# Splits read from PSUM, a negation from raw weights, and one scaling per conv block in a one-core decoder trunk

## The chip, the cores and the metric

The kernel runs on one core of one Trainium2 chip. The metric is device time in microseconds for one launch; the kernel before takes 1084.95 us (median of three runs, 1084.92 to 1085.11).

The core has five engines that run their own instruction queues in order: TensorE (matmuls; PE in the profile, PEld its weight loads), VectorE (DVE), ScalarE (ACT), GpSimd (POOL) and SyncE (SP, which here only issues transfers). SBUF is the on-chip memory, PSUM the accumulators that matmuls write.

## The reference

One layer of a decoder trunk on 288 token columns: 256 positions of a new sequence and 8 x 4 new tokens of running sequences.

```python
h = rmsnorm(x, norm1_g)
proj = einsum("btd,de->bte", h, w_in) + b_in          # 2048 -> 3072
a, gate, z = proj[..., :1024], proj[..., 1024:2048], proj[..., 2048:]
u = a * sigmoid(gate)
c = silu(layernorm(depthwise_causal_conv([hist_conv, u], conv_w, conv_b)))   # 31 taps
# pooling: 4 groups of 256 channels with windows 2, 4, 8, 16
d = window_sum([hist_pool, z]) / count - z
p = einsum("btgc,gce->btge", d, pool_w) * pool_scale                         # 256x256 a group
x = x + einsum("btm,md->btd", concat([c, p]), w_out)                         # 2048 -> 2048
f = square(relu(einsum("btd,df->btf", rmsnorm(x, norm2_g), w_ff1)))          # 2048 -> 8192
x = x + einsum("btf,fd->btd", f, w_ff2)                                      # 8192 -> 2048
y = rmsnorm(x, norm_f)
```

The last 30 conv inputs and 15 pooling inputs of each sequence are outputs too.

## The kernel before, in words

Channels lie on the 128 partitions, the 288 tokens along the free dimension (`T`). Every matmul is 128x128 weights by 128x288 activations in fp32r, a shortened fp32. To keep the precision, each operand is held as two parts, `hi` (the value rounded to fp32r) and `lo` (value minus `hi`), and each product is made of three matmuls: hi by hi, lo by hi, hi by lo. TensorE does 8176 matmuls, and everything else has to make operands in time.

**Weights.** `load` brings a block of 1024 rows by 256 columns as two raw tiles of 4 k blocks each (here called quarters, since two blocks, so four such tiles, make one column pair of 2048 rows). A quarter serves 24 matmuls. `split_part` (L254) makes `hi` and `lo`. `hi` is a copy on ScalarE (L260). `lo` is made in one of three ways, by the letters in `WAYS` (L73), one letter per quarter:

- "V": VectorE subtracts `hi` from raw (L265).
- "G": GpSimd does, in two halves of 128x512 (L269).
- "D": ScalarE writes the negated `hi` into `lo` (L262), and then a transfer from DRAM that adds to its destination brings raw once more (L263). GpSimd issues these transfers.

There are 6 raw tiles and 5 pairs of `hi` and `lo` tiles, used in turn: a quarter is split when the quarter five earlier has been used up by TensorE.

**Order.** `SEQUENCE` (L38) sets the order of the first stage: c0 to c7 are the eight conv column pairs, p3 to p0 the projections of the four pooling groups, P3 to P0 the pooling products of 12 matmuls each. TensorE runs them in the order written: c0 to c4, p3, c5, p2, P3, c6, p1, P2, p0, c7 with P1 inside, then the first columns of w_out with P0 inside, and so on to the feed-forward matrices. A c or p block is 96 matmuls. The order on the other engines is laid out by a planner that simulates durations when the kernel is built and lets ready work of higher rank go first; the conv taps (L459, 31 multiply-adds per block on VectorE, with products for the new tokens on GpSimd, L463) have the lowest rank. Each queue then runs in that fixed order.

**A conv block** (`conv_pair`, L429): both PSUM halves are scaled by the norm's factor `rb` (L434), the gate half goes through the sigmoid (L436), and u is formed (L438). **A pooling group** (`pool_group`, L476): the projection is scaled (L482) and biased on ScalarE (L485, L486), GpSimd adds shifted copies to get window sums `s` (L491) and forms the difference for the new tokens (L497, L498), VectorE the one for the sequence (L500); then `d` is split into `dh` (ScalarE, L502) and `dl` (VectorE, L503). `pool_products` (L509) multiplies them by the pool weights and splits the result again (L514, L515).

**The `ms` tile.** `ms()` hands out one PSUM tile of two banks with a single buffer: each user waits until the one before has been read. Before the change its users around the pooling are only the four pooling products, and the sums of the norms.

`pool_weights` (L375) loads and splits the 256x256 weights of one group; it is called one group ahead of its use, at the end of the block before on TensorE.

Of the kernel before, what the change touches and what calls it, by code (L numbers as in the profile page):

```python
# [9 lines left out]
F32 = mybir.dt.float32  # L10
# [6 lines left out]
P = 128  # L17
# [9 lines left out]
PH = 15  # L27
# [42 lines left out]
TURN = "110100" * 4 + "01" * 6 + "1100" * 3  # L70


WAYS = {"c2": "GVGV", "c3": "GDGG", "c4": "GGGD", "c5": "GDGD", "c6": "GDGV", "c": "GGGV", "p0": "GDVG", "p": "GDDG", "w0": "GV", "w": "GG", "ff": "VV"}  # L73


VEC = (("norm1_g", 16), ("b_in", 24), ("conv_b", 8), ("ln_g", 8), ("ln_b", 8), ("pool_scale", 8), ("norm2_g", 16), ("norm_f", 16))
# [10 lines left out]
def trunk_kernel(ctx: ExitStack, tc: tile.TileContext, io):  # L87
# [18 lines left out]
    def nm(s):  # L106
        seen[s] = seen.get(s, 0) + 1
        return f"{s}{seen[s]}"
# [25 lines left out]
    def f32(t):  # L134
        return t.bitcast(F32)
# [118 lines left out]
    def split_part(raw, src, hi, lo, way):  # L254

        nc.scalar.copy(hi, raw)  # L260
        if way == "D":
            nc.scalar.activation(lo, f32(hi), AF.Copy, scale=-1.0)  # L262
            added.append(nc.gpsimd.dma_start(lo, src, accum_op=ALU.add))  # L263
        elif way == "V":
            nc.vector.tensor_tensor(lo, raw, f32(hi), op=ALU.subtract)  # L265
        else:
            for j in range(0, raw.shape[1], 2):
                with tc.issue_after(pooled[-1].ins) if pooled else nullcontext():
                    nc.gpsimd.tensor_tensor(lo[:, j : j + 2, :], raw[:, j : j + 2, :], f32(hi[:, j : j + 2, :]), op=ALU.subtract)  # L269
# [27 lines left out]
    def gemm(banks, rhs, m_outer=False, between={}, classes="", by_part=False, gets=None, pairs=None, late=0):  # L297


        n = len(rhs)  # L300
        gets = gets or ready.pop(0)
        todo, begins = [], {}
        if by_part:
            for k in range(0, n, 2):
                sets = [range(len(banks))] if k else [range(2), range(2, len(banks))]
                for last, ms_ in enumerate(sets, 1 - len(sets)):
                    for part, (w, x) in enumerate(((0, 0), (1, 0), (0, 1))):
                        if last == 0:
                            begins[len(todo)] = (k, None, k + 1)[part]
                        todo += [(k + (1 - d if x else d), m, w, x) for m in ms_ for d in range(2)]  # L310
        else:
            pairs = pairs or [(k, m) for k in range(0, n, 2) for m in range(len(banks))]
            if m_outer:
                pairs.sort(key=lambda km: km[1])
            for k, m in pairs:
                begins[len(todo)] = (k, m) if m else k
                todo += [(k + d, m, w, x) for d, w, x in ((0, 0, 0), (1, 0, 0), (0, 1, 0), (1, 1, 0), (1, 0, 1), (0, 0, 1))]
        todo[:late] = sorted(todo[:late], key=lambda p: p[2])
        head = todo[: len(classes)]
        for j, c in enumerate(classes):  # L320
            todo[j] = next(p for p in head if c == "." or (p[0] + p[3]) % 2 == int(c))
            head.remove(todo[j])
        ends = {m: [f(j for j, p in enumerate(todo) if p[1] == m) for f in (min, max)] for m in range(len(banks))}
        ahead = None
        for j, (k, m, w, x) in enumerate(todo):
            if begins.get(j) in between:
                ahead = between[begins[j]]()
            with tc.issue_after(ahead.ins) if ahead is not None and not chain else nullcontext():
                last = mm(banks[m][:, :T], gets[k // 8](k % 8, m)[w], rhs[k][x], start=j == ends[m][0], stop=j == ends[m][1])
        ready.extend(itertools.islice(weights, 1))  # L330
        return last.ins

    def bank2():
        return acc.tile([P, 2, 512], F32, name=nm("ac"), tag="ac")

    def each(bk):
        return [bk[:, m, :] for m in range(2)]
# [36 lines left out]

    def pool_weights(g):  # L375
        raw, (hi, lo) = load_pool(g), spl()
        split_part(raw[:, 0:2, :], None, hi[:, 0:2, :], lo[:, 0:2, :], "V")
        return lambda k, m: columns(hi, lo, k, m)

    def weight_groups():  # L380
# [41 lines left out]

    def conv_products(i, **kw):
        history(i)
        banks = each(bank2())
        gemm(banks, hx, **kw)
        return banks

    def conv_pair(i, banks):  # L429
        up = u_all[:, i, 0:UO]  # L430
        us = samples(u_all[:, i, UO:UL], US)
        ta, gate = [b[:, :T] for b in banks]
        for b in (gate, ta):
            nc.vector.tensor_tensor(b, b, rb, op=ALU.mult)  # L434
        tg = tmpp.tile([P, 2, T], F32, name=nm("tg"), tag="ag", bufs=2)[:, 0, :]
        nc.scalar.activation(tg, gate, AF.Sigmoid, bias=v("b_in", 8 + i))  # L436
        for out, a, b in ((up[:, CH:UO], ta[:, :SEQ], tg[:, :SEQ]), (us[:, :, CH:US], samples(ta[:, SEQ:T], NS), samples(tg[:, SEQ:T], NS))):
            nc.vector.scalar_tensor_tensor(out=out, in0=a, scalar=v("b_in", i), in1=b, op0=ALU.add, op1=ALU.mult)  # L438
        if i % 2 == 0:
            cs.append(actp.tile([P, 2, T], F32, name=nm("c"), tag="c", bufs=4))  # L440
        while waiting:
            taps(*waiting.pop())
        if i in (2, 3):
            waiting.append((i, up, us))
        else:
            taps(i, up, us)
# [24 lines left out]
                    nc.gpsimd.tensor_tensor(sum_c[:, 0, :], sum_c[:, 0, :], part, op=ALU.add)  # L471


    dd = {}

    def pool_group(g):  # L476
        nc.sync.dma_start(z_all[:, 2 * g : 2 * g + 2, ZO:ZL], io["hist_p"][:, 2 * g : 2 * g + 2, :])
        bk = bank2()
        gemm(each(bk), hx)
        z = z_all[:, 2 * g : 2 * g + 2, :]  # L480
        tz = tmpp.tile([P, 2, T], F32, name=nm("tz"), tag="ag", bufs=2)
        nc.vector.tensor_tensor(tz, bk[:, :, :T], both(rb), op=ALU.mult)  # L482
        for m in range(2):
            b_in = v("b_in", 16 + 2 * g + m)
            nc.scalar.activation(z[:, m, PH:ZO], tz[:, m, 0:SEQ], AF.Identity, bias=b_in)  # L485
            nc.scalar.activation(samples(z[:, m, ZO:ZL], ZS)[:, :, PH:ZS], samples(tz[:, m, SEQ:T], NS), AF.Identity, bias=b_in)  # L486
        s, w = z, 1
        while w < WINDOWS[g]:
            s2 = tmpp.tile([P, 2, ZL], F32, name=nm("s"), tag="s", bufs=2)
            for m in range(2):  # L490
                nc.gpsimd.tensor_tensor(s2[:, m, 2 * w - 1 :], s[:, m, 2 * w - 1 :], s[:, m, w - 1 : ZL - w], op=ALU.add)  # L491
            s, w = s2, 2 * w
        d = tmpp.tile([P, 2, T], F32, name=nm("d"), tag="ag2", bufs=2)
        first_sums = s[:, :, PH : PH + w - 1]
        nc.gpsimd.tensor_tensor(first_sums, first_sums, rcnt[:, None, w - 2 : 2 * w - 3].to_broadcast([P, 2, w - 1]), op=ALU.mult)
        news = [x[:, :, ZO:ZL].rearrange("p m (b t) -> p m b t", t=ZS)[:, :, :, PH:] for x in (s, z)]
        nc.gpsimd.tensor_scalar(news[0], news[0], 1.0 / w, None, op0=ALU.mult)  # L497
        last = nc.gpsimd.tensor_tensor(d[:, :, SEQ:T].rearrange("p m (b t) -> p m b t", t=NS), news[0], news[1], op=ALU.subtract)  # L498
        newest[g] = last
        nc.vector.scalar_tensor_tensor(out=d[:, :, 0:SEQ], in0=s[:, :, PH:ZO], scalar=1.0 / w, in1=z[:, :, PH:ZO], op0=ALU.mult, op1=ALU.subtract)  # L500
        dh, dl = act2("dx", tag="p", bufs=4)
        nc.scalar.copy(dh, d)  # L502
        nc.vector.tensor_tensor(dl, d, f32(dh), op=ALU.subtract)  # L503
        dd[g] = dh, dl
# [12 lines left out]

    for i in range(2):
        history(i)
    pair0 = each(bank2())  # L520
    pair1 = [cvp.tile([P, 512], F32, name=nm("ac"), tag="cv") for m in range(2)]

    def first_row():
# [2 lines left out]
    chain.append(gemm(pair0 + pair1, hx, between={15: first_row}, classes="01" * 18 + TURN, by_part=True))  # L526
    third = conv_products(2, classes=TURN)
    nc.gpsimd.memset(z_all[:, :, 0:PH], 0.0)
    conv_pair(0, pair0)
    conv_pair(1, pair1)  # L530
    conv_pair(2, third)
    def ahead(n):

        while len(ready) < n + 1:
            ready.extend(itertools.islice(weights, 1))
        return ready.pop(n)

    for kind, i in SEQUENCE[3:-1]:
        if (kind, i) == ("P", 1):
            continue  # L540
        if i == 7:
            pooled.append(newest[1])
        if kind == "c":
            conv_pair(i, conv_products(i, classes=TURN if i == 5 else "", **(dict(gets=ahead(1), between={8: lambda: pool_products(1)}) if i == 7 else {})))
        elif kind == "p":
            pool_group(i)
        else:
            pooled.append(newest[i])
            pool_products(i)
    pooled.append(newest[0])  # L550
    proj = [halves(dd[k // 2])[k % 2] for k in korder]
    bks = [bank2() for _ in range(2)]
# [248 lines left out]
```

## Time and profile before

| | |
|---|---|
| median of three runs | 1084.95 us |
| the profiled execution | 1083.8 us |
| its span | 1082.0 us |
| TensorE busy | 1068.6 us (99%) |
| VectorE busy | 632.2 us (58%) |
| ScalarE busy | 484.2 us (45%) |
| GpSimd busy | 179.8 us (17%) |
| granted TensorE clock | 0.998 of full |

The profile is of one execution. Its span runs from the first to the last instruction, and the time of the whole execution lies 1.8 us above it. In rows of a timeline the columns are start and length in us, engine, line, operation, output from inputs, count, and in brackets how long the engine had been idle and what ended that. In rows of stretches they are the stretch, its length, the busy time of each engine with its instructions, the granted clock, the share of the DMA engines and GB/s. In rows that group instructions they are the busy time, the mean in ns, and the idle time ahead. The shares of the span mislead for the early stage: VectorE and GpSimd have most of their work in the first 210 us.

### The profile page before, as it was taken

What the parts mean: (1) busy time and instruction counts of PE and PEld (TensorE: products, weight loads), DVE (VectorE), ACT (ScalarE), POOL (GpSimd) and SP (SyncE); (2) the same over time, 40 slices, a digit from 0 to 9 for tenths busy, and PEclk for the clock granted to TensorE, in tenths of its full rate; (3) what the DMA queues carried; (4) which work ended last, traced back from release to release, by engine and by line L of the source; (5) the groups of instructions that cost most, each with busy time, mean ns of one, the idle gap of its engine ahead of it and who ended that gap; (6) DMA issues with size and microseconds to landing.
All of it is one profiled execution on the core that took longest, in us unless ns stands there. A gap on an engine that the chain in (4) does not pass through costs nothing.

```text
span 1082.0 us, 19548 instructions
## 1 busy us (share of the span) xinstructions
PE 1068.6 (99%) x8176; PEld 1067.0 (99%) x8176; DVE 632.2 (58%) x804; ACT 484.2 (45%) x593; POOL 179.8 (17%) x189
## 2 busy tenths in 40 slices
PE   9999999999999999999999999999999999999996
PEld 8999999999999999999999999999999999999996
DVE  8899998788655544444544444545544445554552
ACT  8655555565544433334443333444433334444441
POOL 1898889612000000000000000000000000000001
PEclk9999999999999999999999999999999999999999
DMA  9898778555555555555555555555555555555522
GB/s 328 279 267 222 198 173 249 189 168 170 170 169 165 174 171 163 174 168 165 175 171 163 173 168 166 173 172 164 172 171 163 173 172 163 172 169 166 172 79 88
DMA packets 59017, 193.34 MB, mean 179 GB/s; under 512 B 6320, under 2 KB 11312, under 8 KB 58928
## 3 DMA queue, kind: packets, MB, share of 16 engines
q1 hardware_dynamic: 56336, 184.35, 54.4%
q0 software_dynamic: 1728, 6.29, 3.2%
q8 instruction: 64, 1.05, 0.4%
q10 hardware_dynamic: 864, 1.44, 0.4%
q14 instruction: 25, 0.20, 0.1%
HBM read 187.78 MB, written 4.28 MB: 177 GB/s over the span
## 4 chain that ended last, share of the span: by engine, by line
PE 75%; issue 20%; DVE 2%; DMA 1%; POOL 1%; ACT 0%; SPq 0%; POOLq 0%; DVEq 0%
PE ac L292 74%; DMA wlo<-in_w 1%; DMA wr<-in_w 1%; DVE pc L459 1%; PE pp L292 0%; POOL wlo L269 0%; DVE wlo L265 0%; POOL s L491 0%; POOL xT L737 0%; DVE dx L503 0%; DVE z_all L409 0%; SPq L191 0%; ACT z_all L407 0%; DVE wlo L360 0%; DVE c L465 0%
## 5 line engine op out<-in xcount | busy, mean ns | idle before, releaser
L260 ACT CAST whi<-wr 128x1024 fp32r<-128x1024 f32 (+1 forms) x332 | 346.7, 1044 | 549.9 <-PE ac L292 538.3
L265 DVE TENSOR_TENSOR wlo<-wr,whi 128x1024 fp32r<-128x1024 f32 x282 | 348.3, 1235 | 348.0 <-ACT whi L260 348.0
L292 PE MATMUL ac<-ax,whi 128*128 128x288 f32 x2048 | 351.0, 292 | 0.0
L292 PE MATMUL ac<-fx,whi 128*128 128x288 f32 x2048 | 350.2, 292 | 0.0
L292 PEld LDWEIGHTS ac<-ax,whi 128*128 128x128 f32 x2048 | 296.1, 187 | 0.0
L292 PEld LDWEIGHTS ac<-fx,whi 128*128 128x128 f32 x2048 | 295.5, 187 | 0.0
L292 PE MATMUL ac<-ax,wlo 128*128 128x288 f32 x1024 | 217.4, 292 | 0.0
L292 PE MATMUL ac<-fx,wlo 128*128 128x288 f32 x1024 | 216.4, 292 | 0.0
L292 PEld LDWEIGHTS ac<-ax,wlo 128*128 128x128 f32 x1024 | 162.6, 187 | 0.0
L292 PEld LDWEIGHTS ac<-fx,wlo 128*128 128x128 f32 x1024 | 162.2, 187 | 0.0
L737 POOL TENSOR_TENSOR xT<-xT,rf 128x288 f32<-128x288 f32 x4 | 3.1, 793 | 799.9 <-ACT rf L741 799.9
L292 PE MATMUL ac<-hx,whi 128*128 128x288 f32 x768 | 131.1, 294 | 1.3 <-DVE hx L354 1.3
L292 PEld LDWEIGHTS ac<-hx,whi 128*128 128x128 f32 x768 | 111.6, 188 | 1.7 <-ACT hx L356 1.5
L269 POOL TENSOR_TENSOR wlo<-wr,whi 128x512 fp32r<-128x512 f32 x76 | 103.7, 1449 | 21.8 <-ACT whi L260 20.3
L459 DVE SCALAR_TENSOR_TENSOR pc<-u_all,vec,pc 128x256 f32<-128x256 f32 x232 | 100.1, 482 | 3.5 <-ACT pc L456 1.9
L292 PE MATMUL ac<-hx,wlo 128*128 128x288 f32 x384 | 80.4, 295 | 2.0 <-DMA wlo<-in_w 1.7
L292 PEld LDWEIGHTS ac<-hx,wlo 128*128 128x128 f32 x384 | 60.7, 188 | 2.7 <-DMA wlo<-in_w 2.2
L292 PE MATMUL ac<-dx,whi 128*128 128x288 f32 x256 | 46.2, 295 | 0.0
L292 PE MATMUL ac<-mx,whi 128*128 128x288 f32 x256 | 44.5, 292 | 0.0
L679 DVE SCALAR_TENSOR_TENSOR t<-ac,r 128x576 f32<-128x576 f32 x32 | 24.2, 758 | 25.4 <-PE ac L292 25.3
L292 PEld LDWEIGHTS ac<-dx,whi 128*128 128x128 f32 x256 | 38.2, 188 | 0.2
L292 PEld LDWEIGHTS ac<-mx,whi 128*128 128x128 f32 x256 | 37.4, 187 | 0.0
(129 smaller groups left out, 541.7 us busy)
## 6 DMA issues: line engine op xcount, KB each, us to landing
wr<-in_w SPq DMA_DIRECT2D x335, 512.0 KB, 3.8
wlo<-in_w POOLq DMA_DIRECT2D x12, 512.0 KB, 7.7
xT<-in_xT SPq DMA_DIRECT2D x8, 288.0 KB, 7.2
wr<-in_w SPq DMA_DIRECT2D x5, 256.0 KB, 4.8
out_u_out<-u_all SPq DMA_DIRECT2D x1, 1208.0 KB, 10.1
u_all<-in_hist_c SPq DMA_DIRECT2D x8, 136.0 KB, 5.8
out_z_out<-z_all SPq DMA_DIRECT2D x1, 668.0 KB, 8.7
z_all<-in_hist_p SPq DMA_DIRECT2D x4, 152.0 KB, 8.4
```

Source lines behind the costliest of these rows:

```text
L260: nc.scalar.copy(hi, raw)
L265: nc.vector.tensor_tensor(lo, raw, f32(hi), op=ALU.subtract)
L269: nc.gpsimd.tensor_tensor(lo[:, j : j + 2, :], raw[:, j : j + 2, :], f32(hi[:, j : j + 2, :]), op=ALU.subtract)
L292: last = nc.tensor.matmul(*args, **kw)
L459: nc.vector.scalar_tensor_tensor(out=dst, in0=up[:, w : w + SEQ], scalar=cwv[:, w : w + 1], in1=pc, op0=ALU.mult, op1=ALU.add)
L679: nc.vector.scalar_tensor_tensor(out=t, in0=bk[:, :, :T], scalar=0.0, in1=both(rows2[0]), op0=ALU.max, op1=ALU.mult)
L737: eng.tensor_tensor(xk, xk, r[:, None, :].to_broadcast([P, n, T]), op=ALU.mult)
```

## The change

It has five parts.

1. In way "D" the negation reads raw and goes ahead of the `hi` copy. It writes the same value, since writing into `lo` rounds to fp32r.
2. c6 loses its own entry in `WAYS` and takes the common "GGGV" for "GDGV": its second quarter goes from "D" to "G".
3. For groups 3, 2 and 1 the pool weights are copied by ScalarE to an `ms` tile as well, and VectorE's subtraction reads that copy. Group 0 stays as it was.
4. The second half of `pool_group` becomes `pool_means`. `d` is an `ms` tile in PSUM. GpSimd leaves the new tokens' difference in place in `s`, ScalarE copies it to `d`, VectorE writes the rest, and both halves of the split read PSUM. `pool_means` is called later than before: group 3 after p2, groups 2 and 1 after the pooling products of the group before, group 0 in c7 behind P1. P1 moves from the 9th to the 5th k block of c7.
5. The conv blocks whose halves share a PSUM tile (all but block 1) scale both in one operation of 128x576.

```diff
-WAYS = {... "c5": "GDGD", "c6": "GDGV", "c": "GGGV", ...}
+WAYS = {... "c5": "GDGD", "c": "GGGV", ...}
@@ split_part
+        if way == "D":
+            nc.scalar.activation(lo, raw, AF.Copy, scale=-1.0)
         nc.scalar.copy(hi, raw)
         if way == "D":
-            nc.scalar.activation(lo, f32(hi), AF.Copy, scale=-1.0)
             added.append(nc.gpsimd.dma_start(lo, src, accum_op=ALU.add))
@@ pool_weights
-        split_part(raw[:, 0:2, :], None, hi[:, 0:2, :], lo[:, 0:2, :], "V")
+        raw, hi2, lo2 = [t[:, 0:2, :] for t in (raw, hi, lo)]
+        if g in (3, 2, 1):
+            whole = ms("pw")[:, 0, :].rearrange("p (k c) -> p k c", k=2)
+            nc.scalar.copy(whole, raw)
+            nc.scalar.copy(hi2, raw)
+            nc.vector.tensor_tensor(lo2, whole, f32(hi2), op=ALU.subtract)
+        else:
+            split_part(raw, None, hi2, lo2, "V")
@@ conv_products
-        banks = each(bank2())
-        gemm(banks, hx, **kw)
-        return banks
+        bk = bank2()
+        gemm(each(bk), hx, **kw)
+        return bk
@@ conv_pair
-        ta, gate = [b[:, :T] for b in banks]
-        for b in (gate, ta):
-            nc.vector.tensor_tensor(b, b, rb, op=ALU.mult)
+        if isinstance(banks, list):
+            ta, gate = [b[:, :T] for b in banks]
+            for b in (gate, ta):
+                nc.vector.tensor_tensor(b, b, rb, op=ALU.mult)
+        else:
+            nc.vector.tensor_tensor(banks[:, :, :T], banks[:, :, :T], both(rb), op=ALU.mult)
+            ta, gate = [banks[:, m, :T] for m in range(2)]
@@ pool_group
-        d = tmpp.tile([P, 2, T], F32, name=nm("d"), tag="ag2", bufs=2)
...
-        last = nc.gpsimd.tensor_tensor(d[:, :, SEQ:T].rearrange("p m (b t) -> p m b t", t=NS), news[0], news[1], op=ALU.subtract)
-        newest[g] = last
-        nc.vector.scalar_tensor_tensor(out=d[:, :, 0:SEQ], in0=s[:, :, PH:ZO], scalar=1.0 / w, in1=z[:, :, PH:ZO], op0=ALU.mult, op1=ALU.subtract)
+        newest[g] = nc.gpsimd.tensor_tensor(news[0], news[0], news[1], op=ALU.subtract)
+        sums[g] = s, z, news[0], 1.0 / w
+
+    def pool_means(g):
+
+        s, z, fresh, scale = sums[g]
+        d = ms("d")[:, :, :T]
+        nc.scalar.copy(d[:, :, SEQ:T].rearrange("p m (b t) -> p m b t", t=NS), fresh)
+        nc.vector.scalar_tensor_tensor(out=d[:, :, 0:SEQ], in0=s[:, :, PH:ZO], scalar=scale, in1=z[:, :, PH:ZO], op0=ALU.mult, op1=ALU.subtract)
         dh, dl = act2("dx", tag="p", bufs=4)
         nc.scalar.copy(dh, d)
         nc.vector.tensor_tensor(dl, d, f32(dh), op=ALU.subtract)
@@ the main order
-    pair0 = each(bank2())
+    first_bank = bank2()
+    pair0 = each(first_bank)
...
-    conv_pair(0, pair0)
+    conv_pair(0, first_bank)
...
+    def last_pool():
+
+        pool_products(1)
+        pool_means(0)
...
-            conv_pair(i, conv_products(i, classes=TURN if i == 5 else "", **(dict(gets=ahead(1), between={8: lambda: pool_products(1)}) if i == 7 else {})))
+            conv_pair(i, conv_products(i, classes=TURN if i == 5 else "", **(dict(gets=ahead(1), between={4: last_pool}) if i == 7 else {})))
         elif kind == "p":
             pool_group(i)
+            if i == 2:
+                pool_means(3)
         else:
             pooled.append(newest[i])
             pool_products(i)
+            pool_means(i - 1)
```

More of the change, by code (lines that the diff above doesn't have):

```diff
@@ L70 @@
 TURN = "110100" * 4 + "01" * 6 + "1100" * 3
-WAYS = {"c2": "GVGV", "c3": "GDGG", "c4": "GGGD", "c5": "GDGD", "c6": "GDGV", "c": "GGGV", "p0": "GDVG", "p": "GDDG", "w0": "GV", "w": "GG", "ff": "VV"}
+WAYS = {"c2": "GVGV", "c3": "GDGG", "c4": "GGGD", "c5": "GDGD", "c": "GGGV", "p0": "GDVG", "p": "GDDG", "w0": "GV", "w": "GG", "ff": "VV"}
 VEC = (("norm1_g", 16), ("b_in", 24), ("conv_b", 8), ("ln_g", 8), ("ln_b", 8), ("pool_scale", 8), ("norm2_g", 16), ("norm_f", 16))
@@ L471, in taps @@
                     nc.gpsimd.tensor_tensor(sum_c[:, 0, :], sum_c[:, 0, :], part, op=ALU.add)
-    dd = {}
+    dd, sums = {}, {}
     def pool_group(g):
```

## The prediction

> **What bounds the kernel now.** I read the page first, then who waited for whom on TensorE, then the chain of waits, then the timelines of the engines around the places the chain named.
>
> ```profile
> span 1082.0 us, 19548 instructions
> PE 1068.6 (99%) x8176; PEld 1067.0 (99%) x8176; DVE 632.2 (58%) x804; ACT 484.2 (45%) x593; POOL 179.8 (17%) x189
> ...
> PE ac L292 <- DMA wlo<-in_w: 1.7, 2, 1.4
> ...
> wlo<-in_w POOLq DMA_DIRECT2D x12, 512.0 KB, 7.7
> ```
>
> TensorE is busy for 99% of the span, and the change neither adds nor removes a matmul. So it can gain only where TensorE waits or runs below its best rate, and lose only where it makes TensorE wait. In the middle of the kernel TensorE waits for one thing: twice, 1.7 us together, for a `wlo` block that an adding transfer completes (way "D"). The chain of waits gives the rate (start, length, instructions):
>
> ```profile
> 119.51 8.72 DMA wlo<-in_w
> ...
> 128.27 9.58 PE ac L292 x70
> 137.85 1.60 PE pp L292 x12
> 139.45 19.20 PE ac L292 x144
> 158.65 1.60 PE pp L292 x12
> 160.25 9.60 PE ac L292 x72
> 169.85 1.60 PE pp L292 x12
> 171.45 28.18 PE ac L292 x216
> ...
> 283.88 572.63 PE ac L292 x4404
> ```
>
> From 283.88 us on, 4404 matmuls take 572.63 us: 130.0 ns each. From 139.45 us, 144 take 19.20 us: 133.3 ns. The timeline of TensorE has both waits:
>
> ```profile
> 112.81 0.68 PE L292 MATMUL ac<-hx,whi 128*128 128x288 f32 x4
> 114.85 0.54 PE L292 MATMUL ac<-hx,wlo 128*128 128x288 f32 x2 [1.37 <-DMA wlo<-in_w]
> ...
> 127.20 0.69 PE L292 MATMUL ac<-hx,whi 128*128 128x288 f32 x4
> 128.27 0.53 PE L292 MATMUL ac<-hx,wlo 128*128 128x288 f32 x2 [0.38 <-DMA wlo<-in_w]
> ...
> 112.00:116.00 4.00, 2.63 (x20) 2.40 (x19) 4.00 (x7) 2.34 (x7) 3.33 (x2) 1.00 0.36 99
> ```
>
> Without the wait, the matmul at 114.85 would have started four matmuls after 112.81, at 113.33: 1.52 us lost. The one at 128.27 was due at 127.73: 0.54 us lost. Between the two starts lie 96 matmuls (70 left of c6, 26 of p1), so from 112.81 to 171.45 us there are 4 + 96 + 322 = 422. At 130.0 ns they are 54.87 us, and they took 58.64. **The excess is 3.77 us: 2.06 at the two waits and 1.71 of slower rate behind them.** The granted clock is 1.00 in the stretch of the wait (third column from the right), so the throttle is not the cause. This 3.77 us is the most I let the change gain.
>
> **The change, part by part.** *c6's second quarter goes from "D" to "G".* The wait at 114.85 is at the third matmul of that quarter (it begins 24 matmuls into c6). Its transfer hung on ScalarE's negation and on POOL's queue:
>
> ```profile
> 104.55 1.05 ACT L262 ACTIVATE wlo<-whi 128x1024 fp32r<-128x1024 f32 x1
> ...
> 105.00 2.20 POOL L463 TENSOR_TENSOR prd<-u_all,vec 128x992 f32<-128x992 f32 x1
> 107.15 0.88 POOL L263 DMA_DIRECT2D wlo<-in_w  x1
> 107.81 2.80 POOL L269 TENSOR_TENSOR wlo<-wr,whi 128x512 fp32r<-128x512 f32 x2
> ...
> L269 POOL TENSOR_TENSOR wlo<-wr,whi x76: 1280/1366/2481, 27.0 to 206.1; 128x512 fp32r<-128x512 f32 x76
> DMA to landing us min/median/max: 6.3/7.7/10.1
> ```
>
> Issued at 107.15 and landing 7.7 us later, it is there at 114.85. As "G" it is two POOL subtractions, 2.73 us by the median and 4.96 by the maximum. After the product at 105.00 (done 107.20) they end between 109.9 and 112.2, before 113.33. The next pair (2.80 us) then ends at 112.7 by the median, where it is due one quarter later, at 116.4. ScalarE loses 1.05 us of negation, POOL 0.88 of issue and gains 2.73. The term is **-1.52 us**, hidden by up to 3.4 us of lead; if POOL runs these later than I put them, the wait returns, at most whole.
>
> *The negation from raw, ahead of the `hi` copy (11 transfers left).* No work is saved. A transfer can be ready one copy (1.05 us) earlier, `hi` comes one negation later, and the raw buffer is held as much longer. The five `hi` buffers let it be written up to four quarters (96 matmuls, 12.5 us) ahead of its use, which hides its delay; without that cover the 1.05 us would fall on TensorE in each such quarter. The other wait is p1's second quarter:
>
> ```profile
> 116.97 1.06 ACT L262 ACTIVATE wlo<-whi 128x1024 fp32r<-128x1024 f32 x1
> ...
> 119.51 0.88 POOL L263 DMA_DIRECT2D wlo<-in_w  x1
> ```
>
> The negation ends at 118.03 and could end at 116.95. TensorE, 1.52 us earlier by the first edit, now wants the block at 127.73 - 1.52 = 126.21. At 8.72 us it must be issued by 117.5, at 7.7 by 118.5. So 1.08 us from the order does not suffice alone if POOL keeps its place in the queue; it does if POOL issues as soon as the negation is done. POOL's order is laid out anew by the planner, and what delayed POOL there was partly VectorE (next edit). I take the wait as gone, **-0.54 us**; the bounds are that, and a wait of up to 126.21 to 128.23, which gives back the 1.52 and the 0.54 together.
>
> *Splits from PSUM, and one scaling per conv block.* VectorE's rows by shape:
>
> ```profile
> L434 DVE TENSOR_TENSOR ac<-ac,rb 128x288 f32<-128x288 f32 x16 | 7.1, 457 | 1.3 <-PE ac L292 1.3
> L503 DVE TENSOR_TENSOR dx<-d,dx 128x576 fp32r<-128x576 f32 x4 | 5.7, 1427 | 0.0
> L265 DVE TENSOR_TENSOR wlo<-wr,whi 128x512 fp32r<-128x512 f32 x4 | 5.6, 1396 | 0.0
> L482 DVE TENSOR_TENSOR tz<-ac,rb 128x576 f32<-128x576 f32 x4 | 3.0, 748 | 0.4 <-PE ac L292 0.4
> L684 DVE TENSOR_TENSOR fx<-f,fx 128x576 fp32r<-128x576 f32 x32 | 24.3, 758 | 2.3 <-ACT fx L683 0.3
> ...
> 120.00:160.00 40.00, 39.62 (x298) 39.39 (x297) 39.65 (x79) 19.74 (x31) 35.42 (x36) 1.00 0.75 193
> ```
>
> L482 reads one operand from PSUM and takes 0.748 us for 576 elements; L503 reads both from SBUF and averages 1.427. With PSUM sources I price the four L503 at 0.748, which frees 4 x 0.68 = 2.7 us. The three pool weight splits at their mean of 1.40 come to about 0.70 (0.748 scaled down to 512 elements is 0.67), freeing 2.1. Fourteen scalings of 0.457 become seven of 0.748: 1.2 us. VectorE gets 6.0 us back in a stretch in which it is busy 39.65 of 40 us. TensorE never waits for VectorE there, so the direct term is **0**. The cover is the conv taps, which fill every gap and are due only at the layer norm. [...]
>
> ScalarE gains three copies of 128x512, four small ones of 64 elements per partition, and the wait for the single `ms` tile:
>
> ```profile
> 110.94 0.35 ACT L461 ACTIVATE prd<-ones,vec 128x32 f32<-128x32 f32 x1 [1.30 <-DVE c L465]
> ...
> 124.47 0.62 ACT L260 CAST whi<-wr 128x512 fp32r<-128x512 f32 x1 [2.10 <-PE ac L292]
> ...
> 130.54 1.80 DVE L503 TENSOR_TENSOR dx<-d,dx 128x576 fp32r<-128x576 f32 x1
> ...
> 149.37 0.74 DVE L503 TENSOR_TENSOR dx<-d,dx 128x576 fp32r<-128x576 f32 x1
> ```
>
> That is 3 x 0.62 + 4 x 0.35 = 3.3 us on an engine busy 19.74 of 40 us. The serious part is order. `ms` now goes d3, P3's products, d2, P2's weights, P2's products, d1, P1's weights, P1's products, d0. P2's weights, cast at 124.47 before, can be copied only once d2 has been split, about 132.3 before (130.54 + 1.80), against their use at 137.85: 5.5 us of lead for 2 us of work. Their raw buffer comes free as much later, and the load six tiles on (c7's first) stands in SP's queue for it, a whole block ahead of its use. P1's weights follow d1's split, done at 150.11. Copies, subtraction and a few taps take 2.0 to 3.5 us more: 152.1 to 153.6. P1's products move four k blocks earlier in c7, to 152.25 + 24 x 0.133 = 155.45. Both ends ride on TensorE's own progress, so a lead of 2 to 3 us stays. Behind the waiting copy on ScalarE stand c7's casts, for which POOL's subtractions wait, and TensorE for those. Term **0**; each us beyond the lead costs one.
>
> *Rate.* The 133.3 ns set in within 2 us of the first wait, and no row says why. If it follows the wait, 1.71 us go with it; if not, none. The long stretch without waits (130.0) is the nearest row for a path without them, but the link is unproven, so I take half: **-0.85 us**.
>
> **Sum:** 1.52 + 0.54 + 0.85 = 2.9 us. The profiled execution took 1083.8 us, its span 1082.0 and 1.8 around it, so it would be 1080.9. The median of the runs lies 1.15 us above the profiled one, at 1084.95, which gives **1082.0**.
>
> **The rivals.**
> A (forecast): both waits go and no new one comes. Gain 2.06 to 3.77, so 1081.2 to 1082.9; chance 0.50. For it: the lead of 3.4 us at c6, and POOL's and VectorE's relief. Against it: every remaining transfer is as tight as the one removed.
>
> B: given back later. TensorE arrives 1.5 us earlier at p1, and its transfer is only 1.06 us earlier, landing at 127.17 against 126.21. A wait of 0.96 remains, the gain is 1.1 and the rate stays slow: 1083.9 (1082.9 to 1084.5); chance 0.25. For it: POOL was issuing behind its own sums, not behind the negation alone.
>
> C: the change does not do what it says. POOL's queue alone sets the second issue, the block lands at 128.23 as before, and all 2.06 us return: 1085.0; chance 0.11. Against it: the pressure of VectorE on POOL drops.
>
> D: slower. The place is p0's second quarter, also "D":
>
> ```profile
> 132.57 1.06 ACT L262 ACTIVATE wlo<-whi 128x1024 fp32r<-128x1024 f32 x1
> ...
> 131.69 2.73 POOL L463 TENSOR_TENSOR prd<-u_all,vec 128x992 f32<-128x992 f32 x1
> ...
> 135.12 0.88 POOL L263 DMA_DIRECT2D wlo<-in_w  x1
> ```
>
> Issued at 135.12 and landing at about 142.8, it is wanted at 139.45 + 26 x 0.133 = 142.9: no slack at all, and after A's gain it is wanted at 140.0. If ScalarE, in order, stands at P2's copy until 132.3 and then does both copies (1.24) before the negation (1.06), that ends at 134.6. Behind one product on POOL (2.73) the issue is at 137.4 and the landing at 145.1 to 147.5. The wait of 5.1 to 7.5 us leaves 2.2 to 4.6 us of loss: 1087.2 to 1089.6, middle 1088.3. It decides from a landing later than 145.1. Against it: the planner may put the negation ahead of the copies, and the first edits pull POOL earlier; chance 0.14. [...]
>
> **How the numbers follow.** The forecast is A's point. The range runs from A's lower end, 1081.1, to 1085.4, which takes in B and C and leaves D and the edges out. What a measurement can tell from no change is 0.2%, 2.17 us: below 1082.78 is faster. That holds most of A (0.45); the rest of A, B and C are the same (0.41); D is slower (0.14).
>
> **What would show it.** Right: no TensorE wait for `wlo` in 105 to 175 us, 11 adding transfers, L503 at 0.75 us four times, and the stretch from c6 to the last pooling product shorter by 2 to 3.8 us. If the rate is tied to the waits, p0's matmuls come at 130 ns. Wrong: a wait in p1's or p0's second quarter (B, C, D), or TensorE standing at the pooling products for `ms`.

## The result and the profile after

The changed kernel takes **1091.6 us** (median of six runs, 1090.81 to 1093.28) against 1084.95 us for the one before, the median of the five of its six runs that lie together (1083.35 to 1085.97; the sixth took 1319.15 us). The ratio of the two kernels is 1.0067, with an interval of 1.0057 to 1.0077 that lies clear of 1: some 6.6 us slower. The forecast of 1082.0 us and its range are missed. The profiled execution took 1091.55 us.

The page of the kernel after, its head and two of its rows:

```profile
span 1089.7 us, 19546 instructions
...
PE 1073.1 (98%) x8176; PEld 1071.1 (98%) x8176; DVE 627.1 (58%) x797; ACT 483.7 (44%) x599; POOL 178.2 (16%) x190
...
L293 PE MATMUL ac<-hx,wlo 128*128 128x288 f32 x384 | 82.1, 300 | 5.2 <-DMA wlo<-in_w 5.1
...
wlo<-in_w POOLq DMA_DIRECT2D x11, 512.0 KB, 9.3
```

There are 11 adding transfers, as announced, and TensorE waits 5.1 us for them, where it waited 1.7 before. The timeline of TensorE shows where:

```profile
128.59 0.53 PE L293 MATMUL ac<-hx,wlo 128*128 128x288 f32 x2 [0.45 <-DMA wlo<-in_w]
...
147.87 0.85 PE L293 MATMUL ac<-hx,wlo 128*128 128x288 f32 x2 [4.63 <-DMA wlo<-in_w]
```

The wait in c6 is gone. The one in p1's second quarter is still there (0.45 against 0.38), and p0's second quarter, which did not wait before, now waits 4.63 us. The chain of waits leads back to the issue of that block's transfer:

```profile
119.24 9.31 DMA wlo<-in_w
...
133.94 3.90 issue
137.83 0.02 POOLq L270
137.85 9.98 DMA wlo<-in_w
147.82 0.04 issue
147.87 15.30 PE ac L293 x94
163.17 1.60 PE pp L293 x12
...
291.59 572.63 PE ac L293 x4404
```

From 147.87 us, 94 matmuls take 15.30 us, 163 ns each, against 133 in the next row. The stretches of 4 us (busy time of PE, PEld, DVE, ACT and POOL, then the granted clock) say why:

```profile
144.00:148.00 4.00, 0.13 (x1) 0.13 (x1) 4.00 (x11) 0.33 (x2) 3.84 (x7) 0.84 0.98 311
148.00:152.00 4.00, 4.00 (x17) 4.00 (x18) 4.00 (x10) 0.64 (x1) 0.77 (x1) 0.50 0.15 60
152.00:156.00 4.00, 4.00 (x27) 4.00 (x26) 1.22 (x3) 1.54 (x2) 1.32 (x2) 0.81 0.00 0
156.00:160.00 4.00, 4.00 (x32) 4.00 (x32) 2.95 (x8) 1.05 (x1) 3.28 (x3) 1.00 0.92 309
```

After the idle time the granted clock is 0.50: 17 matmuls in 4 us instead of 30, 240 ns from one to the next. The measured cost is about 2.5 us: the quarter took 10.50 us against 3.20 before, and of the 7.30 more, 4.79 are the wait (4.92 us from the start of one matmul to the next, where 0.13 is usual).

Set side by side at the starts of the quarters (first matmul of each in the trace), the time is lost and won as follows:

| stretch on TensorE | before, us | after, us | difference |
|---|---|---|---|
| up to c2 | 33.17 | 33.87 | +0.70 |
| c2 to the start of p2 | 62.74 | 63.00 | +0.27 |
| p2 to c6's second quarter | 17.16 | 18.05 | +0.88 |
| c6's second quarter | 4.80 | 3.20 | -1.60 |
| c6's third to p0's first | 24.62 | 24.70 | +0.08 |
| p0's second quarter | 3.20 | 10.50 | +7.30 |
| p0's third | 3.20 | 3.30 | +0.09 |

Together +7.7 us, the difference of the spans, and nothing is added behind p0. The first row is not put down to the change: that stretch lies from 0.03 us below to 1.21 above the one before in the profiles below, with no edit that goes with it.

ScalarE, GpSimd and VectorE ahead of the late issue, from their timelines:

```profile
131.86 1.06 ACT L262 CAST whi<-wr 128x1024 fp32r<-128x1024 f32 x1 [1.70 <-issue]
132.82 0.63 ACT L519 CAST dx<-d 128x576 fp32r<-128x576 f32 x1
135.02 1.05 ACT L262 CAST whi<-wr 128x1024 fp32r<-128x1024 f32 x1 [1.57 <-PE ac L293]
135.98 0.58 ACT L381 COPY pw<-wr 128x512 f32<-128x512 f32 x1
136.49 1.06 ACT L261 ACTIVATE wlo<-wr 128x1024 fp32r<-128x1024 f32 x1
```

```profile
137.85 0.90 POOL L264 DMA_DIRECT2D wlo<-in_w  x1 [3.91 <-ACT wlo L261]
```

```profile
133.76 0.74 DVE L520 TENSOR_TENSOR dx<-d,dx 128x576 fp32r<-128x576 f32 x1
...
136.59 0.69 DVE L383 TENSOR_TENSOR wlo<-pw,whi 128x512 fp32r<-128x512 f32 x1 [0.91 <-ACT pw L381]
```

The negation of p0's second quarter (L261) starts at 136.49; before, it started at 132.57. It comes after its own `hi` copy (131.86), after the next quarter's (135.02) and after P2's weight copy into `ms` (135.98), though the source has it ahead of its `hi` copy. GpSimd stands idle 3.91 us for it. ScalarE's laid-out order, with the numbers of the tiles, shows that this is the plan (42 is P2's weight tile, 44 p0's second quarter; left the line, right the tile written; a conv tap, the only other work here, is left out):

```
after                                 without the weight copies (E1)
L262 CAST     whi43                   L262 CAST     whi43
L516 COPY     d2                      L516 COPY     d2
L262 CAST     whi44                   L261 ACTIVATE wlo44   <- negation
L519 CAST     dx2                     L262 CAST     whi44
L262 CAST     whi45                   L519 CAST     dx2
L381 COPY     pw2                     L262 CAST     whi45
L261 ACTIVATE wlo44   <- negation     L262 CAST     whi46
L262 CAST     whi46
```

My theory after the result: the `lo` tiles are five buffers handed out in turn, so `wlo44` is handed out only after `wlo42`, P2's. P2's subtraction (L383) waits for the copy `pw2`, which waits for the one `ms` tile until `d2` is split (L520, 133.76). So the negation, which needs neither, is laid out behind the copy. In the execution the queue keeps that order even though the copy itself does not wait: ahead of it, whi45 stands 1.57 us for TensorE. The rival theories: GpSimd's queue or the transfers themselves are late (the order does not matter); or `d` in PSUM is at fault and not the copies; or p0's quarter is merely too tight for way "D".

### The profile page after: what moved, and what is told of

Its sections match the earlier page's. It is cut to its first block, busy times and chain, and to the rows that moved or that the text cites. A ratio compares the mean times of both kernels' runs of the same rounds, so it can differ in the third digit from the quotient of the medians.

```text
span 1089.7 us, 19546 instructions
## 1 busy us (share of the span) xinstructions
PE 1073.1 (98%) x8176; PEld 1071.1 (98%) x8176; DVE 627.1 (58%) x797; ACT 483.7 (44%) x599; POOL 178.2 (16%) x190
## 3 DMA queue, kind: packets, MB, share of 16 engines
q8 instruction: 64, 1.05, 0.4%
## 4 chain that ended last, share of the span: by engine, by line
PE 73%; issue 21%; DMA 3%; POOL 2%; DVE 0%; POOLq 0%; ACT 0%
PE ac L293 72%; DMA wlo<-in_w 3%; POOL wlo L270 1%; DMA wr<-in_w 1%; POOL s L503 0%; PE pp L293 0%; DVE pc L471 0%; POOL xT L763 0%; PE norm L293 0%; POOL wlo L264 0%; POOLq L813 0%; DVE ac L445 0%; DVE xT L736 0%; POOL sum_c L480 0%; ACT whi L352 0%
## 5 line engine op out<-in xcount | busy, mean ns | idle before, releaser
L262 ACT CAST whi<-wr 128x1024 fp32r<-128x1024 f32 x329 | 344.6, 1047 | 544.3 <-PE ac L293 530.1
L266 DVE TENSOR_TENSOR wlo<-wr,whi 128x1024 fp32r<-128x1024 f32 (+1 forms) x279 | 342.8, 1229 | 348.0 <-ACT whi L262 348.0
L293 PE MATMUL ac<-hx,whi 128*128 128x288 f32 x768 | 133.9, 299 | 1.3 <-DVE hx L355 1.3
L293 PEld LDWEIGHTS ac<-hx,whi 128*128 128x128 f32 x768 | 114.6, 193 | 1.7 <-ACT hx L357 1.6
```

What stands on the lines that cost most here:

```text
L293: last = nc.tensor.matmul(*args, **kw)
```

## The experiments

All kernels of this section compute the whole reference. Each ratio is to the kernel before, run on the same chip beside it.

**E1 and E2: without the weight copies, and without P2's alone.**

```diff
-        if g in (3, 2, 1):
+        if g in ():          # no_weight_copies, no_weight_copies_2
+        if g in (3, 1):      # p2_weights_from_sbuf
```

> The changed kernel with no pool weights copied to ms (all four groups subtracted from SBUF as before); d stays in ms. Theory: besides the 7.3 us of p0's second quarter, the small late transfers of p2 (1.0 us) go too, since those stand behind P3's copy that waits on ScalarE for its raw load: 1083.0 to 1083.5 us. Rival (p2's late transfers come from the negation order or the scaling): p2's loss of 0.5 to 1 us stays and the time is like that of the kernel with only P2's copy undone, 1084.3 us.

> The changed kernel with one edit: P2's weights are subtracted from SBUF again, without the copy to the ms tile; P3's and P1's stay as changed. Theory (ms chain): the 4.6 us wait in p0's second quarter comes from P2's copy, which stands behind d2's split in ms and holds back the negation of that quarter; without it the wait and the half clock behind it go, 7.3 us: 1084.3 us, and the negation comes within 2 us of the quarter five earlier being used up (near 132). Rival (negation order or POOL's queue): the wait stays, 1091 to 1092 us.

Without any copy the kernel takes **1081.13 us**, ratio 0.9968 (0.9959 to 0.9978), 1.9 us below the range that I had expected. Without P2's alone it takes 1084.53, ratio 0.9997 (0.9987 to 1.0007), as expected. Taken out in this order, P2's copy costs 7.1 us (1091.6 to 1084.5) and the other two 3.4. The shares are not independent: p2 with P3's products is 2.2 us longer in E2's profile than in that of the kernel after. The negation and the issue without copies, on ScalarE's and GpSimd's timelines:

```profile
129.64 1.05 ACT L261 ACTIVATE wlo<-wr 128x1024 fp32r<-128x1024 f32 x1
```

```profile
89.89 0.84 POOL L264 DMA_DIRECT2D wlo<-in_w  x1
...
134.11 0.92 POOL L264 DMA_DIRECT2D wlo<-in_w  x1
```

The negation is 6.85 us earlier, the issue 3.74, and no matmul from c6 on waits for a `lo` block of an adding transfer (in c3 two start late, by 0.3 us together). The chain of this kernel:

```profile
111.09 24.96 PE ac L293 x192
136.05 1.56 PE pp L293 x12
137.61 15.60 PE ac L293 x120
153.21 1.56 PE pp L293 x12
154.77 12.48 PE ac L293 x96
```

From c6 to P0 every matmul takes 130.0 ns. From the start of p2 to the end of P0, 552 matmuls, it needs 71.76 us where the kernel before needed 75.38: the excess that the prediction put at 3.77 us is gone, the rate's part with the rest.

What P3's copy does is seen without P2's. ScalarE and GpSimd in p2_weights_from_sbuf, and its row of TensorE's waits:

```profile
87.04 0.59 ACT L381 COPY pw<-wr 128x512 f32<-128x512 f32 x1 [4.50 <-DMA wr<-in_w]
...
132.20 1.06 ACT L261 ACTIVATE wlo<-wr 128x1024 fp32r<-128x1024 f32 x1
```

```profile
88.75 2.55 POOL L270 TENSOR_TENSOR wlo<-wr,whi 128x512 fp32r<-128x512 f32 x2 [6.02 <-issue]
```

```profile
PE ac L293 <- DMA wlo<-in_w: 2.2, 2, 1.8
```

P3's copy stands at the head of ScalarE's queue 4.50 us for a load that has not landed. The casts behind it are late, GpSimd idles 6.02 us, p2's adding transfers are issued that much later, and TensorE waits 1.75 us at 101.34 and 0.43 at 105.23. In the kernel after, the same copy (at 86.42) waits 3.13 us, p2's first transfer goes out at 92.34 against 89.89 without copies, and p2 loses most of the 0.88 us of the table.

**E3: the `lo` tile of P2 handed out early.** The copies stay; two elements of `lo` are written ahead of the copy (and overwritten later), so that the tile is handed out before `ms` comes free.

```diff
             whole = ms("pw")[:, 0, :].rearrange("p (k c) -> p k c", k=2)
+            if g == 2:
+                nc.scalar.copy(lo2[:, 0:1, 0:2], raw[:, 0:1, 0:2])
             nc.scalar.copy(whole, raw)
```

> The changed kernel with one instruction more: two elements of P2's lo tile are written by a tiny ScalarE copy ahead of the copy to ms (and written over later), so that the tile is handed out before d2's split is done. Theory: the lo tiles are handed out in turn, and p0's second quarter's negation, two tiles later, waited for P2's tile to be handed out, which waited for the copy to ms. Then the negation comes at about 132, the 4.6 us wait in p0's second quarter goes, and the time is that of the kernel with P2's weights from SBUF, 1084.5 us (P3's copy still costs its part). Rival (the copy's own time on ScalarE, or its raw tile held longer, delays the negation): the wait stays above 3 us, 1089 to 1092 us.

1085.50 us, ratio 1.0007 (0.9997 to 1.0016). ScalarE's timeline, and TensorE's:

```profile
129.47 1.06 ACT L261 ACTIVATE wlo<-wr 128x1024 fp32r<-128x1024 f32 x1 [0.68 <-PE ac L293]
...
133.90 0.58 ACT L383 COPY pw<-wr 128x512 f32<-128x512 f32 x1
```

```profile
136.88 0.54 PE L293 MATMUL pp<-dx,whi 128*128 128x288 f32 x2 [0.78 <-DVE wlo L385]
```

P2's copy is still there and still goes through `ms`, only the hand-out differs, and the negation moves ahead of it, from 136.49 to 129.47. p0's wait is gone (the profiled execution took 1083.63 us, one of the shorter ones of this kernel). This decides for the in-turn hand-out and against GpSimd's queue, the transfer and the quarter's tightness. It also shows that the `ms` chain is tight by itself: here P2's product waits 0.78 us for the subtraction that follows the copy.

**E4 to E6: `d` in SBUF.** All three take `d` out of the `ms` chain. E4 leaves the copies as they are, E5 takes them away too, and E6 puts them behind the `hi` copies.

```diff
-        d = ms("d")[:, :, :T]                                                # E4, E5, E6
+        d = tmpp.tile([P, 2, T], F32, name=nm("d"), tag="ag2", bufs=2)
@@ pool_weights, E5
-        if g in (3, 2, 1):
+        if g in ():
@@ pool_weights, E6
-            nc.scalar.copy(whole, raw)
-            nc.scalar.copy(hi2, raw)
+            first = nc.scalar.copy(hi2, raw)
+            with tc.issue_after(first.ins):
+                nc.scalar.copy(whole, raw)
```

> The changed kernel with d in an SBUF tile again; the three weight copies stay in ms. Theory: P2's copy no longer stands behind d2's split, so the negation of p0's second quarter is early and its wait goes, while P3's copy still blocks ScalarE until its raw load lands: 1084 to 1085 us. Rival (the weight copies cost by themselves, wherever they stand): 1088 us or more.

> The changed kernel with neither the weight copies nor d in ms: what is left is the negation order, c6's way G, one scaling per conv block, and the later place of the pooling means. By the prediction the VectorE time that PSUM sources save is worth nothing on TensorE's path: 1081.1 us as with d in ms. Rival (VectorE's waits for GpSimd delay what ScalarE and GpSimd do for the adding transfers): waits come back, 1082 to 1083 us.

> The changed kernel with d in SBUF and each weight copy to ms issued after the hi copy of the same weights, which waits for a free hi tile and so comes long after the raw load. Theory: the copies cost only where they stop ScalarE's queue, P3's for its raw load and P2's for ms; here neither does: 1081 to 1081.7 us, with no wait for wlo in p2. Rival (the copies cost by themselves): 1084 us or more.

E4: 1084.63 us, ratio 1.0005 (0.9995 to 1.0014). E5: 1082.68, ratio 0.9984 (0.9974 to 0.9994). E6: 1083.33, ratio 0.9992 (0.9982 to 1.0001). So the copies alone, without `d` in the same chain, do not bring the 6.6 us, and `d` alone (E1) does not either: it takes both in the one tile. In E4 p0 has no wait; p1's second quarter waits 1.05 us. E6 and E5 are 0.65 us apart by the medians and their intervals overlap, so whether copies that hold nothing up cost anything is not shown.

E5 and E6 miss what I expected of them: E5 lies in the rival's range, 1.55 us above E1 (on another chip), and E6 1.6 us above its own range. In E5's profile p1's second quarter takes 3.39 us where it takes 3.12 in E1, and from there to P0 the matmuls come at 133.3 ns: together 1.3 us of the 1.9 by which the two spans differ. In E6 the same quarter waits 0.48 us. Its transfer is issued at 119.14 in E5 and 118.02 in E6, against 117.64 in E1. That points at a gain from `d` in PSUM, but with two kernels on two chips it is not settled.

**E7 and E8: parts 2 and 1 on the kernel before.**

```diff
-WAYS = {... "c5": "GDGD", "c6": "GDGV", "c": "GGGV", ...}     # E7, E8
+WAYS = {... "c5": "GDGD", "c": "GGGV", ...}
@@ split_part, E8
+        if way == "D":
+            nc.scalar.activation(lo, raw, AF.Copy, scale=-1.0)
         nc.scalar.copy(hi, raw)
         if way == "D":
-            nc.scalar.activation(lo, f32(hi), AF.Copy, scale=-1.0)
```

> The kernel before with one edit: c6's second quarter by way G. The prediction's first term alone: the wait of 1.52 us in c6 goes. If nothing takes it back: 1083.4 us, and down to 1081.7 if the 130 ns rate stays too. Rival B of the prediction: TensorE comes 1.5 us earlier to p1's second quarter, whose transfer is issued as before, and waits there for up to 2.06 us: 1084.5 to 1085.0 us.

> The kernel before with two edits: c6's second quarter by way G, and the negation from raw ahead of the hi copy. The prediction's first two terms: 2.06 us, 1082.9 us, down to 1081.2 with the rate. If the order is worth nothing because POOL's queue sets the issue of p1's transfer, it is as the kernel with the first edit alone.

E7, c6's quarter alone: 1086.22 us, ratio 1.0017 (1.0008 to 1.0026), a little slower, where I had a gain. Its wait in c6 is gone, but the profile (of the longest of ten executions, 1087.89 us) has four others: two in p3, and the two largest in the second quarters of p1 and p0. TensorE's timeline, GpSimd's issues of the two transfers, and the stretches around the first:

```profile
130.06 0.54 PE L292 MATMUL ac<-hx,wlo 128*128 128x288 f32 x2 [2.06 <-DMA wlo<-in_w]
...
146.79 0.53 PE L292 MATMUL ac<-hx,wlo 128*128 128x288 f32 x2 [2.07 <-DMA wlo<-in_w]
```

```profile
120.67 0.89 POOL L263 DMA_DIRECT2D wlo<-in_w  x1
...
138.48 0.87 POOL L263 DMA_DIRECT2D wlo<-in_w  x1
```

```profile
126.00:130.00 4.00, 1.99 (x16) 1.76 (x14) 3.93 (x8) 0.64 (x2) 3.31 (x5) 1.00 1.06 225
130.00:134.00 4.00, 3.94 (x29) 3.94 (x30) 3.96 (x10) 2.46 (x5) 2.21 (x3) 1.00 0.83 251
```

p1 and p0 each wait 2.1 us. This looks like rival B, in which TensorE comes 1.5 us earlier to a transfer issued as before, but it is not: the waits in p3 have used up the gain, and TensorE starts p1's second quarter at 127.57 against 127.47 before. It is the blocks that come later. p1's transfer is issued at 120.67 against 119.51, and from there to the start of the matmul that waits for it are 9.39 us against 8.76; p0's is issued at 138.48 against 135.12. What in the new plan delays them no run isolates. E8, with the negation first as well: 1082.70 us, ratio 0.9981 (0.9972 to 0.9991), and of these four waits only one of 0.32 us, at 78.98, is left.

**E9: the old order of the negation, without the copies.** The reverse of part 1, in the version of E1; E1 is repeated beside it as no_weight_copies_2.

```diff
-        if way == "D":
-            nc.scalar.activation(lo, raw, AF.Copy, scale=-1.0)
         nc.scalar.copy(hi, raw)
         if way == "D":
+            nc.scalar.activation(lo, f32(hi), AF.Copy, scale=-1.0)
```

> The same kernel as no_weight_copies (the changed kernel with all pool weights subtracted from SBUF), once more, to be compared with the two below on one chip. Both views: 0.3% below the kernel before, 1081 to 1081.7 us if the gain is real and not of that one chip.

> The same, with the old order in way D: the hi copy first, then the negation from hi. The prediction's second term alone: the transfers are ready 1.05 us later, so waits come back at p1's and p0's second quarters: 1 to 3 us slower, 1082.5 to 1084.5 us. Rival (POOL's queue sets the issue whatever the negation does): no difference, 1081.1 us.

The repeat gives 1080.98 us, ratio 0.9970 (0.9959 to 0.9981). The old order gives 1088.39 (median of nine runs, 1085.33 to 1089.98), ratio 1.0032 (1.0020 to 1.0043): the order is worth 7.4 us by the medians, far more than the 0.54 of the prediction and the 1 to 3 that I expected here. TensorE's timeline and stretches:

```profile
128.81 0.53 PE L292 MATMUL ac<-hx,wlo 128*128 128x288 f32 x2 [1.77 <-DMA wlo<-in_w]
```

```profile
128.00:132.00 4.00, 3.19 (x16) 3.19 (x17) 3.93 (x11) 2.10 (x3) 1.71 (x4) 0.70 0.93 242
132.00:136.00 4.00, 4.00 (x28) 4.00 (x28) 3.80 (x9) 2.63 (x4) 4.00 (x4) 0.87 0.21 73
```

p1's second quarter waits 1.77 us and the clock is halved behind it, for part of each of the two stretches: 3.6 us lost there, and the rate of 133.3 ns up to P0 adds 1.0. The profiled execution took 1085.83 us, among the shortest of this kernel; what the longer ones lost more is in no trace.

**E10: two scalings again, without the copies.** The branch for lists (two multiplications of 128x288) is taken for every conv block.

```diff
-        if isinstance(banks, list):
+        if True:
+            banks = banks if isinstance(banks, list) else each(banks)
```

> The same, with the conv halves scaled in two operations again. By the prediction the 1.2 us that the single scaling saves on VectorE are worth nothing on TensorE's path: 1081.1 us within 0.6. Rival (VectorE's time counts through the casts and sums behind it): 1082 us or more.

1081.02 us, ratio 0.9972 (0.9960 to 0.9983), beside 1080.98: the single scaling has no gain that shows.

**E11: p0's second quarter on GpSimd,** the copies kept.

```diff
-"p0": "GDVG"
+"p0": "GGVG"
```

> The changed kernel, weight copies and all, with p0's second quarter by way G for D: the late transfer is not there at all. Theory: its wait and the half clock behind it were 7.3 us of the loss: 1084.3 us within 1. Rival (whatever holds up the negation holds up GpSimd's subtraction as much, since it too writes a lo tile that is handed out after P2's): a wait of some us stays, 1087 to 1091 us.

1091.70 us, ratio 1.0063 (1.0046 to 1.0080): no gain, against my own expectation. p0's wait goes, and one of the same size comes in c7's first quarter; p2 takes 1.6 us longer too. The timelines of TensorE, GpSimd and ScalarE:

```profile
158.68 0.85 PE L293 MATMUL ac<-hx,wlo 128*128 128x288 f32 x2 [4.54 <-POOL wlo L270]
```

```profile
155.67 1.74 POOL L503 TENSOR_TENSOR s<-z_all 128x422 f32<-128x422 f32 x2 [8.05 <-ACT z_all L498]
157.36 8.46 POOL L270 TENSOR_TENSOR wlo<-wr,whi 128x512 fp32r<-128x512 f32 x6
```

```profile
156.10 0.58 ACT L381 COPY pw<-wr 128x512 f32<-128x512 f32 x1
```

GpSimd idles 8.05 us, then does p0's window sums, then c7's subtraction. c7's `lo` tile is 48; tile 47 is P1's, whose copy `pw3` (156.10) waits for `d3`'s split. It is the same pattern one pooling group later. That the hand-out holds tile 48 back is read from the order; no run with P1's tile claimed early was made.

## Why the prediction was wrong

**The step that failed** is the term 0 for ScalarE's copies and the order of `ms`. The prediction asked whether P2's weights come in time for P2's product, found 5.5 us of lead for them, and there it was right: P2's product starts at 138.02 us without a wait. It named c7's casts as what stands behind a waiting copy. What stands there is the negation of p0's second quarter, laid out behind the copy because its `lo` tile is handed out after P2's (E3). The term is not 0 but 10.5 us for the three copies (1091.6 to 1081.1), 7.1 of it P2's. Of the rest E2 shows the main cause: P3's copy stands 4.50 us for its raw load at the head of ScalarE's queue, a wait that the prediction does not consider.

**Rival D** had this place and this chain: negation done at 134.6, issue at 137.4, landing at 145.1 to 147.5, a wait of 5.1 to 7.5. Measured are 137.55, 137.85, 147.82 and 4.63. It got a chance of 0.14, on the argument that the planner may put the negation ahead of the copies, and it would, were the tile free to be handed out. Its price of 1088.3 is 3.3 us too low. It kept the gains of the forecast, where p1's wait and the rate stayed, and left the clock out of the sum; the 2.5 us of half clock is the largest item missing.

**c6's second quarter,** -1.52: right, -1.60. But alone it does not make the kernel faster (E7): waits come up in p3, p1 and p0 instead. In p1 the cause is a block that lands later, not, as in rival B, TensorE coming earlier.

**The negation first,** -0.54: right in sign, much too small. It was sized by the one wait left before; it also prevents waits that the other edits bring with their new plans (3.5 us from E7 to E8, 7.4 in E9). In the kernel after p1's wait stays, since its transfer goes out at 119.24 there and at 117.64 without the copies.

**VectorE,** 0: right for the scaling, and not settled for the rest. Rows of the kernel after, grouped by shape:

```profile
L445 DVE TENSOR_TENSOR ac<-ac,rb 128x576 f32<-128x576 f32 x7 | 5.3, 764 | 3.6 <-PE ac L293 3.5
...
L520 DVE TENSOR_TENSOR dx<-d,dx 128x576 fp32r<-128x576 f32 x4 | 3.0, 747 | 1.0 <-ACT dx L519 1.0
...
L383 DVE TENSOR_TENSOR wlo<-pw,whi 128x512 fp32r<-128x512 f32 x3 | 2.1, 689 | 3.7 <-ACT pw L381 3.7
```

0.747 for the split of `d` (priced 0.748), 0.689 for the weights (0.70), 0.764 for a scaling (0.748). The instructions became as short as worked out. E10 shows that the shorter scaling buys no time; what the shorter split of `d` buys E5 leaves open, and the shorter split of the weights was paid for with the copies.

**The rate,** half of 1.71: in these runs it follows the waits whole. Without them 552 matmuls take 130.0 ns each (E1); after a wait of 0.32 us and a matmul late by 0.15 ahead of it (E8), or matmuls late by 0.2 us together (E5), the 133.3 ns are back, up to c5 or up to the first columns of w_out, where the kernel passes `classes=TURN`. Why it ends there no run shows.

The sum of the forecast, 1082.0, is within 1 us of what the change gives without its weight copies (1081.13 and 1080.98). That is partly luck: the gain there is 3.5 to 3.6 us, nearly the whole ceiling of 3.77 and not the 2.9 of the sum, and the order of the negation gave far more of it than its 0.54.

## What to carry to other kernels

When an edit puts a wait on an instruction, look not only at who needs its result, but at which buffers it takes its turn in: a tile of a rotating set that is handed out late holds back the tiles after it, and with them work that depends on neither the wait nor its cause (in E3 the negation moved from 136.49 to 129.47 us). Price a wait on TensorE with the clock behind it (here some 2.5 us behind 4.63). And an edit that removes one of several tight waits lays out the rest anew: here it was worth something only together with the edit that made the other transfers less tight.

## What the runs showed of the hardware

The clock does not go by the length of the wait alone. It was halved behind 4.63 us (the kernel after), 4.54 us (E11) and 1.77 us (E9), and it stayed at 1.00 behind waits of 2.06 and 2.07 us (E7, in the stretches of 4 us from 126 to 134 and from 142 to 154). Half clock lasted from 146.72 to 153.54 us in the kernel after, from 156.32 to 163.15 in E11 (worked out from clocks of 0.54 and 0.61 in the 4 us from 156 and from 160) and from 129.62 to 133.04 in E9 (from 0.70 and 0.87 above): twice, twice and once the same 3.41 us. In the kernel after each change lies a whole number of such stretches behind the time from which matmuls first come at the full rate: that is 10.18 us (15 matmuls in the 3.41 us ahead of it, 28 in those behind), and the two changes come 136.54 and 143.36 us later, 40 and 42 of them. The 3.41 us ahead of the three halvings held 0.00, 1.23 and 1.64 us of work on TensorE (the kernel after, E11, E9). In all three full clock came back behind 3.41 us with work throughout; a stretch with 2.26 us of work (the kernel after, 146.72 to 150.13) did not bring it back. How little work a halving takes is not shown: at the end of the kernel after, 3.41 us with 2.07 us of work (1078.56 to 1081.97) are followed by half clock too.

The granted clock alone does not tell a slower TensorE either: in E2's profile its mean is 0.946, and it reads 0.95 in each of the three stretches of 4 us from 96 to 108 us, but 18 matmuls from 96.31 to 98.65 us come at 130.0 ns each, and the 2048 of `ac<-ax,whi` take 292 ns each, as in the kernel before with its mean of 0.998.

An adding transfer of 512 KB has a median of 9.3 us from issue to landing in the kernel after and 7.7 in the one before. Among the 11 of E5 it took from 5.5 to 10.3 us, among the 11 of the kernel after from 8.2 to 11.5. For p0's second quarter, from the issue to the start of the matmul that waits, it was 10.02 us in the kernel after (137.85 to 147.87) and 8.31 in E7 (138.48 to 146.79): a place with a microsecond or two of slack cannot be sized from the profile of another kernel.
